# A two-layer attention and gated-delta backbone on one core: the block inversion in two parts, the second layer's modulation moved to the first layer's MLP, and small matmuls kept together by tile

## The chip, the cores and the metric

The kernel runs on one core of one Trainium2 chip. The metric is the device time of one execution in microseconds, median of several runs. Five engines work side by side, each through its own instruction list in order: TensorE (PE, matmuls and transposes; PEld are its weight loads), VectorE (DVE), ScalarE (ACT), GpSimd (POOL) and SyncE (SP), which here issues nearly all DMAs. They wait for one another through semaphores.

## The reference, cut to what matters

A batch of 512 latent tokens (a 64-wide grid) and 256 context tokens, both 1024 wide, passes through two layers:

```python
def hybrid_layer(x, cx, cond, cond_ctx, ...):
    sh_a, sc_a, gt_a, sh_m, sc_m, gt_m = ada_mod(cond, w_mod, b_mod)   # silu(cond) @ w_mod + b_mod, (1024) -> 6 x 1024
    csh_a, ..., cgt_m                  = ada_mod(cond_ctx, w_mod, b_mod)
    a_qkv, a_z, a_beta, a_alpha, b_qkv, c_qkv = split_cols(modulate(x, g_attn, sh_a, sc_a) @ w_in)
    ...                                                     # the same for the context
    o_a, oc_a = gdn_mixer(...)                              # gated delta rule, 8 heads, both directions, chunks of 64
    o_b, oc_b = global_gqa(...)                             # 4 heads, all keys
    o_c, oc_c = window_gqa(...)                             # 4 heads, banded, with sinks
    x = x + gt_a * (jnp.concatenate([o_a, o_b, o_c], axis=-1) @ w_out)
    x = x + gt_m * sq_relu_mlp(modulate(x, g_mlp, sh_m, sc_m), w_mlp_in, w_mlp_out)   # relu(h @ w1)^2 @ w2, 4096 wide
    ...                                                     # the context too, in the first layer only

def gated_delta_chunked(q, k, v, g, beta, s0):              # per direction and head, chunk by chunk
    low = jnp.where(idx[:, None] > idx[None, :], einsum(kb, kc) * decay, 0.0)          # 64 x 64
    sol = triangular_solve(eye + low, rhs, lower=True, unit_diagonal=True)             # u, w
    v_new = u_i - w_i @ s;  s_new = s * exp(gl_i) + ke_i.T @ v_new                     # serial over the chunks
    o_i = q_i @ s + a_i @ v_new
```

The modulation of a layer is a product of a vector (two of them: latent and context condition) with a 1024 x 6144 matrix, 24 MB of weights. The triangular solve is done through the inverse of `eye + low`.

## The kernel before

**Recording and planning.** The Python code doesn't issue instructions. Each call such as `nc.tensor.matmul` records an operation with the tiles that it reads and writes (`Program.add`, L353). `Program.layout` (L428) then plans: it gives each operation a cost and a rank (the longest priced path from it to the end of the program), and runs a list scheduler over the five engines. At each step the engine that is free first takes, among its operations whose inputs are ready, the one of highest rank, if a buffer is free for it. `Program.issue` (L639) emits the instructions in the order found. So the order on each engine, DMA issues included, follows from costs, ranks and buffer counts, and a small edit can move instructions anywhere. All instructions are emitted from one line, L683, so the trace is read by tile names, not by lines.

**Buffers.** `KINDS` (L36) lists the kinds of tiles, with columns, whether the type is fp32r, and five counts of slots: kept all the time, in region X in phases 0 and 1 of a layer, in region X in phase 2, and the same for region Y. Phase 0 of a layer is its input projection, phase 1 the scans and attention, phase 2 the output projection and the MLP. A region is opened for its next phase when all tiles of the one before are done. `sm` holds a 128x1024 piece (512 KB) of `w_mod`: two slots, in phases 0 and 1 alone. `x` and `h` (the residual and the hidden activations) live in region X of phase 2. `ps` and `pu` are the eight PSUM banks, five and three. `st` and `w` are raw weights and their split into two fp32r halves (ACT makes the high part, DVE the low part).

**Dense work.** Each projection multiplies with three fp32r products (`mm3`, L796): 24 matmuls of 512 columns for the latent tokens and 24 of 256 columns for the context per 128x1024 weight piece. The trace has them as `ps<-b,w` (projections, first MLP matrix), `ps<-w,b` (head projections) and `ps<-h,w` (second MLP matrix).

**Modulation** (`mod_steps`, L822). The six vectors of a layer are computed in three steps r = 0, 1, 2 of two vectors each. A step loads 16 pieces of `w_mod` into `sm` and runs four matmuls per piece, 128 rows by 32 columns (`ps<-sm,cs`, eight records per piece), into one `ps` bank; then ACT copies the bank, PE transposes it and DVE adds the bias. Step 0 is needed by a layer's first norm, steps 1 and 2 by its output projection and its MLP. Before the change, `run` records steps 1 and 2 of layer l, and step 0 of layer l + 1, after the attention of layer l, that is in phase 1.

**The scan.** For each of two head groups g there are six units u, each one 128-row system per direction. `system` (L1466) builds A and stores it to memory; `invert` (L1500) loads the 16x16 diagonal blocks of all six units as rows of one tile (96 partitions: 16 rows per unit), and inverts them together on DVE by 22 pairs of a product (`u<-iv,iv`) and a reduction (`iv<-u`); the result goes to memory as `Z`. `pre` (L1530) loads a unit's part of `Z` (`q<-Z`), which POOL spreads into a tile `s`, and completes the inverse by small matmuls of 32x32 and 64x32 blocks (`pu<-s,u`, `pu<-s,s`). Two `scan_step`s per unit follow, a serial chain of matmuls of 64x64 blocks (`pu<-v,u`, `pu<-u,kv`, `pu<-u,kaq`) and DVE, ACT and POOL work. `key_products` (L1443) makes the 64x64 products of keys and queries (`ps<-g`, `ps<-g,g`).

**What sets the order around the change.** `units` (L1730) records system 0 to 5, one inversion, then pre and scan unit by unit. PE takes matmuls by rank, one at a time: two products that go to different tiles, and are ready together, alternate.

Of the kernel before, what the change touches and what calls it, by code (L numbers as in the profile page):

```python
# [33 lines left out]


KINDS = {  # L36
# [267 lines left out]
PE, ACT, DVE, POOL, SP = range(5)  # L304
# [3 lines left out]
WINDOW = 4096 / 1.2  # L308
COLD = 0.36
WARM = 0.66  # L310
TABLES = {AF.Exp: 0, AF.Tanh: 0, AF.Ln: 1}


class Program:
# [113 lines left out]
    def layout(self):  # L428
        ops = self.ops
# [10 lines left out]
        for k, l in chains.items():  # L440
            n = KINDS[k][2] + KINDS[k][3] + max(KINDS[k][5:])
# [43 lines left out]
        clock, avail, future = [0.0] * 5, [[] for _ in range(5)], [[] for _ in range(5)]  # L485
        parked = {k: [] for k in KINDS}
        queues, front, order, table = 0.0, 0, [], 0
        warm, work, spill, window = False, 0.0, 0.0, 0
        done = bytearray(len(ops) + 1)
        for o in ops:  # L490
            if not o.wait:
                heapq.heappush(future[o.eng], (0.0, o.n))
# [40 lines left out]
        while len(order) < len(ops):  # L533
# [5 lines left out]
            if best is None and early:  # L539
                n = heapq.heappop(early)[1]  # L540
# [5 lines left out]
            t, e = best  # L546
            now = max(now, t)
            while future[e] and future[e][0][0] <= t:
                n = heapq.heappop(future[e])[1]
                heapq.heappush(avail[e], (-ops[n].rank, n))  # L550
            n = heapq.heappop(avail[e])[1]
            o = ops[n]
            if longest - o.rank > AHEAD[e] and n != front and n not in forced and any(
                    x.slot is None and x.kind in HOARD for x in o.tiles):
# [23 lines left out]
            o.start = t  # L578
            end = t + o.dur
            if e == PE:  # L580

                w = int(t / WINDOW)
                while window < w:
                    warm = work > (COLD if warm else WARM) * WINDOW
                    work, window = spill, window + 1
                    spill = 0.0
                if not warm:
                    end += o.dur
                d = (end - t) * o.dense
                over = min(1.0, max(0.0, end - (w + 1) * WINDOW) / (end - t))  # L590
                work, spill = work + d * (1 - over), spill + d * over
# [10 lines left out]
            for s in o.succs:  # L602
                q = ops[s]
# [24 lines left out]
            while early and (longest + early[0][0] <= AHEAD[ops[early[0][1]].eng] or early[0][1] == front):  # L628
                n = heapq.heappop(early)[1]
# [79 lines left out]
class Model:  # L709
# [236 lines left out]
        return xs, y  # L946

    @job("mlp")
    def mlp(self, L, who, xs, y, W, after=None):

        acc = dict.fromkeys(who)
        for q in range(4):
            hid = {i: [] for i in who}
            for s in range(KT):
                ps = self.fm_steps(self.weight(W.pop(0)), y, who)
                for i in who:
                    n = TOKENS[i]
                    r = self.g()
                    self.act(r[:, :n], ps[i][:, :n], AF.Relu)
                    hi, lo = self.pair("hid", i, s, "h")  # L960
                    self.act(hi, r[:, :n], AF.Square)
                    self.mul(r[:, :n], r[:, :n], r[:, :n])
                    self.tt(lo, r[:, :n], hi.bitcast(F32), ALU.subtract)
                    hid[i].append((hi, lo))
            for j in range(KT):
                ps = self.fm_steps(self.weight(W.pop(0)), hid, who)
                for i in who:
                    self.residual(L, xs[i], j, ps[i], i, 40)
                    if q == 3:
                        if after and i == LAT:  # L970
                            after(j, xs[i][j])
                        if not L.last:
                            acc[i] = self.norm_add(acc[i], xs[i][j], TOKENS[i])
        return acc
# [754 lines left out]

    def units(self, L, g, us):  # L1730
        if us and us[0] == 0:
            for u in range(6):
                self.system(L, u, g)
            self.invert(L, g, range(6))
        for u in us:
            self.pre(L, u, g)
            for st in (2 * u, 2 * u + 1):
                self.p.lead = LEAD[g]
                self.scan_step(L, g, st)
            ts = {1: () if L.last else (4, 5), 4: (1, 2), 5: (0, 3)}.get(u, ())  # L1740
            if ts:
                self.finish(L, ts, g)

    def run(self):
# [25 lines left out]
        for L in layers:  # L1770
# [14 lines left out]
            for i in reversed(who):  # L1785
                for nm, row in (("B", 4), ("C", 6)):
                    self.attention(L, nm, nm == "C", row, i)
            self.mod_steps(L, (1, 2))
            if not L.last:
                self.mod_begin(layers[L.l + 1])  # L1790
                self.mod_steps(layers[L.l + 1], (0,))
            self.enter(3 * L.l + 2)
            W = self.out_mlp_weights(L.l)
            xs, y = self.out_proj(L, who, W, x2 if L.last else self.a["xT"])
            if L.last:
                self.mlp(L, who, xs, y, W, lambda j, x: nc.sync.dma_start(self.out[:, j, :], x))
            else:
                acc = self.mlp(L, who, xs, y, W)
                x2 = self.p.tile("dram x2", (P, KT, NL), F32, None)
                for k in range(KT):  # L1800
                    nc.sync.dma_start(x2[:, k, :], xs[LAT][k])
                y = {i: self.norm_end(acc[i], layers[L.l + 1], 0, i, xs[i]) for i in (CTX, LAT)}
# [19 lines left out]
```

## Time and profile before

| | us |
|---|---|
| median of 3 runs (2345.0 to 2347.67) | 2345.96 |
| the profiled execution | 2335.23 |
| its span, first to last instruction | 2333.4 |
| PE busy | 2119.1 (91% of the span) |
| DVE busy | 1214.4 (52%) |
| ACT busy | 878.4 (38%) |
| POOL busy | 358.0 (15%) |
| mean granted TensorE clock | 0.929 of full speed |

The program passes, in order, through phases 0 and 1 of the first layer (to about 710 us of the span), its output projection and MLP (to about 1320), phases 0 and 1 of the second layer (to about 1910), and its output projection and MLP. In the rows further down a window is "start:end, length, busy time of each engine (instructions), granted TensorE clock, busy share of the DMA engines, GB/s". A line of a timeline is "start, length, engine, line, operation, output<-inputs, shapes, type, count", and in brackets the idle time of the engine before it and who ended it. Equal instructions that follow each other are merged in one line. Lengths of matmuls overlap, so what a piece of work costs PE is read as the distance from its start to the next line's start.

### The profile page before, as it was taken

What the parts mean: (1) busy time and instruction counts of PE and PEld (TensorE: products, weight loads), DVE (VectorE), ACT (ScalarE), POOL (GpSimd) and SP (SyncE); (2) the same over time, 40 slices, a digit from 0 to 9 for tenths busy, and PEclk for the clock granted to TensorE, in tenths of its full rate; (3) what the DMA queues carried; (4) which work ended last, traced back from release to release, by engine and by line L of the source; (5) the groups of instructions that cost most, each with busy time, mean ns of one, the idle gap of its engine ahead of it and who ended that gap; (6) DMA issues with size and microseconds to landing.
All of it is one profiled execution on the core that took longest, in us unless ns stands there. A gap on an engine that the chain in (4) does not pass through costs nothing.

```text
span 2333.4 us, 45381 instructions
## 1 busy us (share of the span) xinstructions
PE 2119.1 (91%) x18584; PEld 1690.0 (72%) x18584; DVE 1214.4 (52%) x2481; ACT 878.4 (38%) x1717; POOL 358.0 (15%) x392
## 2 busy tenths in 40 slices
PE   5899999679989899999999888989869988999999
PEld 2687788446657788888888767678636766878777
DVE  4668547765653632332333485757754655334333
ACT  4736325336432521312222363543425444222321
POOL 0133323432320000000000012244411310000000
PEclk9888899779998999999999997979769989999999
DMA  7267425894763121221221327466675532322322
GB/s 276 83 183 201 118 77 160 250 296 123 213 214 115 46 73 57 77 72 46 73 66 66 95 78 195 130 186 200 204 207 160 165 97 69 102 91 99 100 91 82
DMA packets 250224, 305.49 MB, mean 131 GB/s; under 512 B 97952, under 2 KB 172704, under 8 KB 250016
## 3 DMA queue, kind: packets, MB, share of 16 engines
q1 hardware_dynamic: 250016, 302.59, 43.0%
q8 instruction: 146, 2.39, 0.4%
q14 instruction: 62, 0.51, 0.1%
HBM read 246.32 MB, written 56.20 MB: 130 GB/s over the span
## 4 chain that ended last, share of the span: by engine, by line
PE 72%; DVE 9%; DMA 8%; ACT 4%; issue 3%; SPq 2%; POOL 2%; DVEq 0%; ACTq 0%; POOLq 0%
PE ps L683 65%; PE pu L683 7%; DVE g L683 3%; DMA sm<-w_mod 2%; SPq L683 2%; ACT g L683 2%; DVE t L683 2%; DVE u L683 2%; ACT L683 1%; DVE w L683 1%; POOL u L683 1%; DMA u<-kk 1%; DMA u<-xT 1%; DMA st<-w_qkv 1%; ACT u L683 1%
## 5 line engine op out<-in xcount | busy, mean ns | idle before, releaser
L683 PE MATMUL ps<-b,w 128*128 128x512 f32 (+1 forms) x3936 | 832.2, 363 | 22.4 <-ACT b L683 10.6
L683 PEld LDWEIGHTS ps<-b,w 128*128 128x128 f32 x3936 | 661.7, 193 | 151.9 <-ACT b L683 13.4
L683 PE MATMUL ps<-h,w 128*128 128x512 f32 (+1 forms) x2304 | 476.0, 356 | 1.9 <-DVE w L683 0.9
L683 PEld LDWEIGHTS ps<-h,w 128*128 128x128 f32 x2304 | 381.3, 188 | 70.7 <-DVE w L683 4.9
L683 ACT ACTIVATE w<-st 128x1024 fp32r<-128x1024 f32 x192 | 198.1, 1055 | 600.9 <-PE ps L683 598.9
L683 DVE TENSOR_TENSOR w<-st,w 128x1024 fp32r<-128x1024 f32 x192 | 234.7, 1250 | 245.0 <-PE ps L683 177.1
L683 ACT ACTIVATE g<-ps 128x512 f32<-128x512 f32 (+4 forms) x334 | 164.7, 514 | 267.9 <-PE ps L683 265.7
L683 DVE SCALAR_TENSOR_TENSOR x<-ps,mod,x 128x512 f32<-128x512 f32 (+1 forms) x120 | 77.3, 659 | 276.7 <-PE ps L683 276.6
L683 PE MATMUL ps<-w,b 128*128 128x256 f32 x1536 | 214.0, 292 | 1.1 <-ACT g L683 0.7
L683 PEld LDWEIGHTS ps<-w,b 128*128 128x128 f32 x1536 | 196.3, 195 | 5.8 <-ACT g L683 1.1
L683 PE MATMUL ps<-sm,cs 128*32 128x256 f32 x688 | 88.6, 465 | 42.0 <-DMA sm<-w_mod 36.3
L683 DVE TENSOR_TENSOR g<-g 128x512 f32<-128x512 f32 (+3 forms) x112 | 57.9, 542 | 125.5 <-ACT h L683 118.9
L683 DVE SCALAR_TENSOR_TENSOR g<-ps,par,g 128x510 f32<-128x510 f32 (+3 forms) x176 | 104.0, 620 | 31.9 <-ACT g L683 31.3
L683 PE MATMUL ps<-cst,g 128*128 128x128 f32 (+1 forms) x502 | 95.7, 307 | 21.2 <-ACT g L683 16.4
L683 POOL MEMSET iv<- 96x64 f32 (+1 forms) x12 | 5.5, 454 | 675.1 <-DVE g L683 657.9
L683 ACT ACTIVATE g<-ps,t 128x256 f32<-128x256 f32 (+2 forms) x144 | 75.2, 529 | 75.8 <-DVE t L683 70.5
L683 PEld LDWEIGHTS ps<-cst,g 128*128 128x128 f32 (+1 forms) x502 | 60.9, 152 | 50.4 <-ACT g L683 28.5
L683 PE MATMUL ps<-g,g 128*64 128x128 f32 (+1 forms) x1056 | 92.1, 294 | 5.7 <-DVE g L683 3.7
L683 DVE TENSOR_REDUCE t<-ps 128x2 f32<-128x512 f32 (+3 forms) x104 | 62.8, 623 | 60.9 <-PE ps L683 58.3
L683 PE MATMUL pu<-u,kaq 64*64 64x64 f32 (+1 forms) x1344 | 90.5, 248 | 2.6 <-DVE u L683 1.7
L683 DVE TENSOR_TENSOR g<-g,g 128x512 f32<-128x512 f32 (+3 forms) x129 | 76.6, 627 | 28.6 <-ACT g L683 24.2
L683 PEld LDWEIGHTS pu<-u,kaq 64*64 64x64 f32 (+1 forms) x1344 | 66.9, 152 | 25.8 <-issue 9.5
(131 smaller groups left out, 2326.8 us busy)
## 6 DMA issues: line engine op xcount, KB each, us to landing
st<-w SPq DMA_DIRECT2D x128, 512.0 KB
sm<-w_mod SPq DMA_DIRECT2D x86, 512.0 KB
st<-w_qkv SPq DMA_DIRECT2D x24, 512.0 KB
st<-w_tm SPq DMA_DIRECT2D x24, 512.0 KB
kv<-kv SPq DMA_DIRECT2D x96, 128.0 KB
u<-gd SPq DMA_DIRECT2D x88, 128.0 KB
u<-kk SPq DMA_DIRECT2D x88, 128.0 KB
kaq<-kq SPq DMA_DIRECT2D x80, 128.0 KB
```

The source lines that it names most:

```text
L683: getattr(engines[o.eng], o.name)(*[real(x) for x in o.args], **{k: real(x) for k, x in o.kw.items()})
```

## The change

Three edits, all in what is recorded and how it is ordered; the computation is the same, and so is the number of matmuls.

1. **Inversion in two parts.** `units` builds the systems of units 0 and 1, inverts them, then builds those of units 2 to 5 and inverts those. Each inversion runs the same 22 pairs on DVE, on 32 and on 64 partitions where it was one on 96.
2. **Second layer's modulation in the first layer's MLP.** `sm` gets one slot in region X of phase 2. The first layer's phase 1 records only its own steps 1 and 2; the second layer's steps 0, 1 and 2 are recorded at the start of the first three quarters of the first layer's MLP. The second layer's phase 1 has none.
3. **Small matmuls of a tile together.** The planner remembers the PSUM tile of the last matmul on PE if that matmul fills less than `FULL` = 0.9 of the array (`dense`: rows of the contraction over 128, times 0.6 for 64 columns or fewer), and takes a ready matmul into the same tile before one of higher rank. The modulation's matmuls have 128 rows and 256 columns, so for them `dense` is 1.0 and the rule doesn't apply.

```diff
-    "sm": (1024, False, 0, 2, 0, 0, 0),
+    "sm": (1024, False, 0, 2, 1, 0, 0),
...
+FULL = 0.9
...
+        group = None
...
             n = heapq.heappop(avail[e])[1]
+            if e == PE and ops[n].args[0].tile is not group:
+
+                d = [x for x in avail[e] if ops[x[1]].args[0].tile is group]
+                if d:
+                    d = min(d)
+                    avail[e].remove(d)
+                    heapq.heapify(avail[e])
+                    heapq.heappush(avail[e], (-ops[n].rank, n))
+                    n = d[1]
             o = ops[n]
...
             if e == PE:
+                group = o.args[0].tile if o.dense < FULL else None
...
-    def mlp(self, L, who, xs, y, W, after=None):
+    def mlp(self, L, who, xs, y, W, after=None, beside=None):
...
             hid = {i: [] for i in who}
+            if beside and q < 3:
+                self.mod_steps(beside, (q,))
...
         if us and us[0] == 0:
-            for u in range(6):
-                self.system(L, u, g)
-            self.invert(L, g, range(6))
+            for part in (range(2), range(2, 6)):
+                for u in part:
+                    self.system(L, u, g)
+                self.invert(L, g, part)
...
-            self.mod_steps(L, (1, 2))
-            if not L.last:
-                self.mod_begin(layers[L.l + 1])
-                self.mod_steps(layers[L.l + 1], (0,))
+            if L.l == 0:
+                self.mod_steps(L, (1, 2))
...
-                acc = self.mlp(L, who, xs, y, W)
+                self.mod_begin(layers[L.l + 1])
+                acc = self.mlp(L, who, xs, y, W, beside=layers[L.l + 1])
```

PE, second layer, where the attention starts (`ps<-a,a` scores, `ps<-cst,g` transposes, `ps<-g,g` outputs) and unit 0 of head group 1 is completed (`pu<-s,u`, 32 matmuls, then `pu<-s,s`). Before:

```order
L683 MATMUL pu_140<-s_14918,u_11614 32x32 x17
L683 MATMUL ps_137<-a_14928,a_11633 128x512 x2
L683 MATMUL ps_139<-cst,g_14917 128x128
L683 MATMUL pu_140<-s_14918,u_11614 32x32 x2
L683 MATMUL ps_136<-g_14916,g_115 64x128 x4
L683 MATMUL pu_140<-s_14918,u_11614 32x32
L683 MATMUL ps_138<-sm_11600,cs 32x256 x4
L683 MATMUL pu_140<-s_11604,s_11603 32x32 x29
```

After, the same unit; its neighbours are now the transposes of the head projections (`ps<-cst,r`):

```order
L696 MATMUL ps_137<-cst,r_11911 128x128 x2
L696 MATMUL pu_142<-s_15825,u_11891 32x32 x32
L696 MATMUL pu_140<-u_15827,kaq_15833 64x64 x7
L696 MATMUL pu_142<-s_11880,s_11879 32x32 x32
L696 MATMUL ps_137<-cst,r_11911 128x128 x4
L696 MATMUL pu_142<-s_15825,u_11891 64x32 x16
```

The 32 matmuls stand in five pieces before and in one after, no modulation is among them, and the unit is completed ahead of the attention, not within it. Counted over the two orders, matmuls into `pu` of 64 rows or fewer stand in 541 pieces before and 313 after (first layer 267 and 152, second 274 and 161), those into `ps` in 309 and 185 (162 and 103, 147 and 82).

PE, first layer's MLP, `h` the hidden activations. Before, dense matmuls alone:

```order
L683 MATMUL ps_138<-h_7273,w_109 128x512
L683 MATMUL ps_137<-h_7269,w_112 128x512
L683 MATMUL ps_135<-h_7267,w_112 128x256
L683 MATMUL ps_139<-h_7266,w_109 128x256
L683 MATMUL ps_135<-h_7267,w_112 128x256
```

After, at the start of modulation step 1 of the second layer, and in step 0:

```order
L696 MATMUL ps_136<-b_7296,w_112 128x512 x2
L696 MATMUL ps_136<-b_7296,w_110 128x512
L696 MATMUL ps_137<-sm_7228,cs 32x256 x4
L696 MATMUL ps_139<-h_7229,w_108 128x512 x2
L696 MATMUL ps_139<-h_7229,w_113 128x512
```

```order
L696 MATMUL ps_138<-sm_7228,cs 32x256
L696 MATMUL ps_139<-b_7290,w_110 128x256
L696 MATMUL ps_135<-b_7293,w_113 128x512
L696 MATMUL ps_138<-sm_7228,cs 32x256
L696 MATMUL ps_139<-b_7300,w_112 128x256
L696 MATMUL ps_138<-sm_7228,cs 32x256
L696 MATMUL ps_139<-b_7300,w_112 128x256
L696 MATMUL ps_135<-b_7293,w_113 128x512
L696 MATMUL ps_138<-sm_7228,cs 32x256
```

48 pieces of `w_mod` pass through the one `sm` slot here. Between one piece's matmuls and the next stand as a rule some 21 dense matmuls of 512 columns, or as much in other widths; in steps 1 and 2 the four of a piece stand together, in step 0 (which begins in the output projection) five pieces are broken up, nine cuts in all.

SP, second layer, head group 1: the store of the inverted blocks (`Z<-iv`) and the loads of the first attention (`a<-kB`). Before:

```order
L683 DMA Z_97<-iv_11632 96x1024
L683 DMA sm_11601<-w_mod 128x1024
L683 DMA kC_103<-r_11635 512x1x128
L683 DMA a_14928<-kB_100 128x2x512
L683 DMA a_14929<-qB_99 128x2x512
L683 DMA a_14930<-kB_100 128x2x512
L683 DMA q_14924<-Z_97 64x8x16 x2
```

After, the first part's store and reload, and (62 rows further on) the attention's loads:

```order
L696 DMA Z_97<-iv_11907 32x1024
L696 DMA iv_11908<-A_95 8x63x16 x3
L696 DMA q_11900<-Z_97 64x8x16 x2
L696 DMA iv_11908<-A_95 8x63x16 x3
L696 DMA q_11901<-Z_97 64x8x16 x2
```

```order
L696 DMA a_15835<-kB_100 128x2x512
L696 DMA kaq_11904<-B_96 64x512
L696 DMA a_15836<-qB_99 128x2x512
```

The first units' blocks are stored 65 rows ahead of the attention's loads, where the one store stood three rows ahead of them.

## Rows read from the trace of the kernel before

**Rows 1.** Windows by stage: length, busy of PE, PEld, DVE, ACT, POOL, clock, DMA, GB/s.

```profile
120.00:400.00 280.00, 262.88 (x2829) 228.86 (x2826) 180.12 (x334) 120.30 (x217) 90.89 (x80) 0.91 0.53 149
400.00:540.00 140.00, 101.67 (x1204) 66.92 (x1204) 91.98 (x251) 54.74 (x147) 51.72 (x50) 0.78 0.89 260
540.00:690.00 150.00, 139.96 (x2610) 99.63 (x2604) 89.81 (x294) 73.62 (x219) 42.77 (x50) 1.00 0.60 179
690.00:710.00 20.00, 9.04 (x57) 3.04 (x58) 5.19 (x23) 3.47 (x7) 1.01 (x2) 0.59 0.80 258
710.00:1320.00 610.00, 603.61 (x3415) 524.64 (x3415) 227.95 (x346) 165.49 (x266) 0.00 (x0) 0.99 0.20 66
1320.00:1690.00 370.00, 321.22 (x3472) 264.38 (x3470) 259.23 (x504) 170.07 (x316) 113.71 (x124) 0.87 0.58 161
1690.00:1740.00 50.00, 29.07 (x210) 14.90 (x209) 27.98 (x74) 10.09 (x23) 10.75 (x10) 0.57 0.73 216
1740.00:1910.00 170.00, 159.01 (x2621) 112.27 (x2613) 95.80 (x317) 84.61 (x246) 38.91 (x45) 0.95 0.47 139
```

**Rows 2.** PE's waits from 690 to 710 us: us in total, times, longest.

```profile
PE ps L683 <- DMA sm<-w_mod: 8.8, 5, 3.7
```

**Rows 3.** The chain that ended last, 685 to 712 us: start, us, what.

```profile
689.69 4.84 DMA sm<-w_mod
...
694.58 1.13 PE ps L683 x8
...
701.76 4.07 DMA sm<-w_mod
```

**Rows 4.** Timeline of PE, first layer, scans and attention.

```profile
665.57 0.63 PE L683 MATMUL ps<-sm,cs 128*32 128x256 f32 x4
666.13 0.68 PE L683 MATMUL pu<-u,kaq 64*64 64x64 f32 x14
...
667.29 0.75 PE L683 MATMUL pu<-s,u 32*32 32x32 f32 x64
667.97 0.33 PE L683 MATMUL ps<-cst,g 128*128 128x128 f32 x1
668.23 0.62 PE L683 MATMUL ps<-sm,cs 128*32 128x256 f32 x2
668.78 0.68 PE L683 MATMUL pu<-v,u 64*64 64x64 f32 x16
```

**Rows 5.** Timeline of PE, second layer, unit 0 of head group 1.

```profile
1739.76 0.42 PE L683 MATMUL pu<-s,u 32*32 32x32 f32 x10 [2.23 <-POOL s L683]
1740.11 1.11 PE L683 MATMUL ps<-cst,g 128*128 128x128 f32 x4
...
1745.66 0.50 PE L683 MATMUL pu<-s,u 32*32 32x32 f32 x34
1746.09 0.73 PE L683 MATMUL ps<-a,a 128*128 128x512 f32 x2
...
1746.86 0.25 PE L683 MATMUL pu<-s,u 32*32 32x32 f32 x4
1747.04 0.66 PE L683 MATMUL ps<-g,g 128*64 128x128 f32 x8
```

**Rows 6.** Windows of the instructions on sm alone: PE, PEld, clock, DMA, GB/s.

```profile
1690.00:1740.00 50.00, 10.76 (x76) 2.27 (x76) 0.57 0.73 216
1740.00:1910.00 170.00, 21.07 (x152) 5.20 (x152) 0.95 0.47 139
```

**Rows 7.** Windows of the instructions on iv alone, the four inversions' sum: DVE, POOL.

```profile
sum 570.00, DVE 77.86 POOL 3.14; mean DVE 19.46 POOL 0.79
```

**Rows 8.** Timelines of SP and POOL, second layer, before unit 0 of head group 1.

```profile
1725.59 0.34 SPq L683 DMA_DIRECT2D Z<-iv  x1
1732.11 3.37 SPq L683 DMA_DIRECT2D q<-Z  x4
```

```profile
1739.10 0.61 POOL L683 TENSOR_TENSOR s<-q,cst 128x256 f32<-128x256 f32 x1 [27.88 <-DMA q<-Z]
```

**Rows 9.** Timeline of PE, where the first layer's output projection starts.

```profile
709.58 35.81 PE L683 MATMUL ps<-b,w 128*128 128x512 f32 x202 [0.79 <-ACT b L683]
```

2 rows, old and new, of the table KINDS are left out of this document.

## The prediction

> **What bounds the kernel now.** I read the windows by stage first [rows 1], then who ends PE's waits, then single lines of the timeline. The kernel has two sorts of stages. In the first layer's output projection and MLP (710 to 1320 us) PE is busy 603.61 of 610 us at a clock of 0.99, so whatever is added to PE there lengthens the run by its own length. In phases 0 and 1 PE is busy 262.88 of 280, 101.67 of 140, 139.96 of 150, 9.04 of 20 us in the first layer, and 321.22 of 370, 29.07 of 50, 159.01 of 170 in the second. So most of these stages is PE's too, but in two holes, at 400 to 540 and 1690 to 1740 us, PE idles for 38 and 21 us and the granted clock falls to 0.78 and 0.57 [rows 1]. The second hole can be followed: DVE's inversion of head group 1 ends, `Z` is stored at 1725.59, reloaded from 1732.11, POOL spreads it at 1739.10 after an idle of 27.88 us [rows 8], and PE takes it at 1739.76 [rows 5]. At 690 to 710 us PE has nothing but the last pieces of `w_mod`; 8.8 us of waiting go to them [rows 2], and the chain that ended last runs through their loads [rows 3].
>
> **Small matmuls together.** What a cut costs is read from the distance to the next start. Unit 0's 64 records of 32x32 products in one piece take 667.97 - 667.29 = 0.68 us; pieces of 10, 34 and 4 take 0.35, 0.43 and 0.18 [rows 4, 5]. A line through these is about 0.17 us per piece and 0.008 us per record. I take 0.2 us per cut, since the 64x64 products are longer at the start (14 records in 0.6 us or less). The orders have 115 cuts fewer into `pu` in the first layer and 113 in the second, 23 us each. Of the 59 and 65 fewer cuts into `ps` most are key products, of which no line here shows the price apart; I take 0.1 us, 6 us each, between 0 and the 0.2 above. Where PE idles a cut costs nothing: PE is busy 0.87 of these stages, less in the holes, so I count three quarters: **-22 us in each layer**. Bounds: 0, if other engines set the pace, and -45, where the clock is at its low level and a cut costs double.
>
> **The modulation taken out.** Step 0 of the second layer leaves the first layer's phase 1, 16 pieces. A piece between other work costs about 0.56 us whether it has 2, 4 or 8 records (666.13 - 665.57, 668.78 - 668.23) [rows 4]. Ten pieces lie in filled stretches: -5.7 us. Six stand at 690 to 710 us, where PE only waits for their loads [rows 2, 3]; but the scan's end, its store and the reload of the mix run at the same time, and the other 32 pieces stay in the phase. Of the 20 us I take half, -10, bounds 0 and -19. In the second layer all 32 leave. Those in the hole (10.76 us busy at 0.57 of the clock) were fillers and are worth nothing; those after 1740 us are 152 records, 19 pieces, 21.07 us busy as an upper bound and 19 x 0.56 = 10.6 as a lower [rows 6]: **-14 us**. What hides behind them: nothing, PE takes the next attention or scan product.
>
> **The modulation put into the MLP.** 48 pieces on a full engine. At the warm clock 0.56 us per piece between other small work [rows 4], 1.13 at the low clock [rows 3]. In the MLP each one stands between dense matmuls, a pair that this trace does not show, so I take 0.75: 36 us. Nine cuts of step 0 at 0.56 add 5 us, three closings (four transposes behind each step) 2 us. Then the loads: with one slot, a piece is loaded only after the matmuls of the one before. A load takes 4.07 to 4.84 us [rows 3]. Meanwhile PE has some 21 dense matmuls; 202 of mixed width took 35.81 us [rows 9], 0.177 each, hence about 0.236 for one of 512 columns and 5.0 us for 21. The two nearly balance, and where an `st` load runs at the same time the load is late; I take 0.1 us per piece, 5 us. **+48 us**, bounds 27 (0.56 each and nothing else) and 130 (2.7 us per piece, the distance of such pieces at 690 to 710 us).
>
> The Trainium skill, "TensorEngine Tiling (Array Packing)", section Key Properties, says that a change of tiling mode drains TensorE. It speaks for the grouping and against these 48 pieces, each of which changes the mode twice. That a piece of 2 records costs as much as one of 8 agrees with it; the page has no price, and the sum would be the same by it, since 0.75 lies above the row's 0.56.
>
> **The inversion in two parts.** It adds 88 pairs of DVE instructions, since an instruction's length follows its columns, and these are the same on 32, 64 or 96 partitions. The four inversions took 77.86 us of DVE [rows 7], so +39 us in each layer, and four more stores, 12 more POOL memsets and their waits, all in engines that are busy under 0.75 of these stages (DVE 259.23 of 370, POOL 113.71 of 370) [rows 1]. DVE also splits the weights for PE in these stages, in order, so a part comes through: I take 6 us of 39 per layer, bounds 0 and 39. In return the first two units need no longer wait for the systems of the other four. In the order of SP the first `Z` of the second layer's head group 1 stands 65 rows ahead of the attention's loads, before it was three, and PE completes unit 0 among the transposes of the head projections. So the scan fills the hole, and what comes next there is the attention, which then runs without it at the end of the phase. Second layer: idle 21 us and 29 us of busy time at 0.57 of the clock, of which I take **-14**, bounds 0 and -35; first layer, where the hole is also a DMA queue at 0.89 [rows 1] and the attention's own chains, **-10** of 38, bounds 0 and -38.
>
> **The sum.** First layer, phases 0 and 1: -22 - 5.7 - 10 - 10 + 6 = -42. MLP: +48. Second layer: -22 - 14 - 14 + 6 = -44. The second MLP is untouched. Together -38 against the profiled execution of 2335, that is 2297; the median of the runs lies 11 us above the profiled one, so 2346 - 38 = **2308 us** for the median after.
>
> **The rivals.** *The loads of the MLP set PE's pace.* If each piece lands 1.5 us behind the matmul that needs it, because the `st` loads share the queue, 48 x 1.5 = 72 us less the 5 counted come on top: -38 + 67 = +29, 2375 us, slower. It decides from 0.9 us per piece on (43 us). For it: a full engine that runs in order, one slot, loads of 4.07 to 4.84 us beside 5.0 us of cover. Against it: a DMA share of 0.20 there [rows 1], and a load that is late only if others run with it. *DVE becomes the bound in phases 0 and 1.* With all 78 us on the path in place of 12, +28, 2374 us. For it, DVE's 74 instructions and 27.98 us in the hole at 1690, just before PE is fed [rows 1]; against it, DVE idles a third of these stages. Half of it on the path gives -11, 2335. *The cuts cost nothing*, because PE's stretches with scans are paced by the chain through DVE and ACT, and the grouping only lets lower ranks pass: the 44 us go, +6, 2352, at the edge of what can be told from no change. For it, the serial scan; against it, 159.01 of 170 us busy. *More than forecast:* the scan fills both holes wholly and the clock stays up: 24 more from the holes, 12 without the DVE toll, 10 on the pieces at 0.56, so -84, 2262 us.
>
> **How the numbers follow.** The forecast, 2262 to 2341, has 0.66. More than that 0.10. No change, within 0.2% (4.7 us, about what a measurement of this kernel tells from none), 0.08: the costless cuts or half of DVE's toll. Slower 0.16: the late loads 0.07, DVE 0.05, the costless cuts with dearer pieces 0.04. So faster 0.76, same 0.08, slower 0.16. A range from 2258 to 2362 leaves out about 0.1 on either side.
>
> **What would show it.** The window of the first MLP longer by 40 to 55 us, with `sm` pieces of 0.56 to 0.8 us between dense matmuls, and PE waiting for `sm` there under 10 us; 50 or more would be the first rival. The hole before the second layer's attention at under 30 us, its scan of head group 1 starting before the first `ps<-a,a`. Small products of a unit in one line of the timeline of 0.6 to 0.7 us. PE's busy time lower by 20 us or more in all. At the end of the first layer's phase 1 no wait for `sm` of 8 us. DVE busy up by about 78 us. Wrong it would be if phases 0 and 1 got no shorter though PE's work in them did: then the waits of PE there name DVE tiles, or the attention stands alone at the end and PE idles.

## The result, and the profile after

The changed kernel takes 2310.94 us (median of 4 runs, 2301.45 to 2314.42), the kernel before 2345.48 beside it. The ratio is 0.985 with an interval of 0.982 to 0.989, so the change is worth 35 us; the forecast was 38. The profiled execution took 2314.42 us, its span 2312.3, at a mean clock of 0.921.

The stage table below carries the rest of this text. A stage ends where a row of PE's timeline says so: "layer 1" runs from the start to the first unbroken `ps<-b,w` of the first output projection, "MLP 1" to the last `ps<-h,w` of the first MLP, "layer 2" to the first `ps<-b,w` of the second output projection, "rest" to the last `ps<-h,w`. Each row is one profiled execution, so a difference carries the scatter of two. The profiled execution of the kernel before is 10 us faster than its median, those of the other kernels lie within 8 us of theirs; the stage "MLP 1" agrees within 1.4 us in all kernels without the move, so the scatter lies in the other stages. Against "before" the rows therefore come out up to 18 us too high in sum, mostly some 10 (-21 here, where the medians give -35).

| kernel | layer 1 | MLP 1 | layer 2 | rest |
|---|---|---|---|---|
| before | 709.6 | 619.2 | 580.6 | 419.4 |
| after | 687.1 | 667.4 | 528.1 | 425.1 |
| difference | -22.5 | +48.2 | -52.5 | +5.7 |
| forecast | -42 | +48 | -44 | 0 |

The windows by stage of the kernel after (columns as in [rows 1]):

```profile
120.00:400.00 280.00, 244.91 (x2953) 211.67 (x2957) 207.78 (x413) 122.38 (x223) 97.13 (x86) 0.88 0.56 158
400.00:540.00 140.00, 101.15 (x1553) 77.49 (x1549) 107.61 (x266) 50.98 (x133) 71.47 (x68) 0.77 0.76 218
540.00:687.00 147.00, 136.22 (x2036) 95.06 (x2036) 90.18 (x308) 80.72 (x237) 28.22 (x32) 0.94 0.61 179
687.00:1354.00 667.00, 657.21 (x3843) 542.26 (x3844) 235.28 (x371) 169.32 (x271) 0.00 (x0) 0.99 0.32 103
1354.00:1720.00 366.00, 314.19 (x3990) 263.45 (x3991) 297.43 (x630) 179.21 (x334) 135.06 (x140) 0.90 0.59 162
1720.00:1770.00 50.00, 34.77 (x684) 26.55 (x680) 30.01 (x83) 13.74 (x38) 15.25 (x19) 0.60 0.57 150
1770.00:1883.00 113.00, 103.53 (x1323) 78.56 (x1323) 71.02 (x252) 70.04 (x209) 23.00 (x25) 0.93 0.26 75
```

Beside [rows 1] three things are to be seen. The MLP is still full: PE is busy 657.21 of 667 us. The first layer's hole at 400 to 540 us is as it was: 101.15 busy of 140 at 0.77, before 101.67 at 0.78. The second layer's hole is narrower and no warmer: 34.77 of 50 at 0.60, before 29.07 at 0.57. Over the whole stages, layer 1 is shorter by 29.5 us of PE's busy time and longer by 7.0 us of its idle time (113.7 before, 120.7 after); layer 2 is shorter by 49.1 us of busy and 3.4 us of idle time (79.9 and 76.5). So nearly all that the change gains there is work of PE, not waiting.

What PE waits for in the first MLP, from the list of its waits (us in total, times, longest); no `sm` is among them:

```profile
PE ps L696 <- ACT b L696: 6.3, 2, 3.6
PE ps L696 <- DVE w L696: 2.0, 3, 0.9
PE ps L696 <- ACT g L696: 1.4, 3, 0.7
PE ps L696 <- DVE amul L696: 0.6, 1, 0.6
```

How a modulation piece lies there, from the timeline of PE:

```profile
706.72 0.64 PE L696 MATMUL ps<-sm,cs 128*32 128x256 f32 x8
707.29 7.50 PE L696 MATMUL ps<-b,w 128*128 128x512 f32 x32
714.72 0.63 PE L696 MATMUL ps<-sm,cs 128*32 128x256 f32 x4
715.27 0.49 PE L696 MATMUL ps<-b,w 128*128 128x512 f32 x1
715.70 0.63 PE L696 MATMUL ps<-sm,cs 128*32 128x256 f32 x4
716.25 0.73 PE L696 MATMUL ps<-b,w 128*128 128x512 f32 x2
```

From start to next start a whole piece (eight records) takes 0.57 us and half a piece (four records, one of the cuts of step 0) 0.55. A dense matmul beside a piece takes longer than one among its like: the lone one between the two halves 0.43 us, the 32 in a row 0.23 each. All instructions on `sm` in this stage, and those on `iv` in the whole run (one window each, PE and DVE busy):

```profile
687.06:1354.50 667.44, 36.18 (x376) 0.99 0.32 103
```

```profile
0.00:2312.00 2312.00, 158.03 (x352) 0.92 0.44 132
```

376 records are 47 pieces, 0.77 us of busy time each with their cuts; the trace has them in 56 rows. The inversions take 158.03 us of DVE where they took 77.86 [rows 7]. The second layer's head group 1: the first row below is unit 0, the first of the first part, to be held against [rows 5]; the other three are unit 2, the first of the second part:

```profile
1682.57 0.75 PE L696 MATMUL pu<-s,u 32*32 32x32 f32 x64
...
1742.42 1.08 PE L696 MATMUL pu<-s,u 32*32 32x32 f32 x64 [1.26 <-POOL s L696]
1743.43 1.11 PE L696 MATMUL pu<-u,kaq 64*64 64x64 f32 x14
1744.47 1.07 PE L696 MATMUL pu<-s,s 32*32 32x32 f32 x64
```

The products stand together, 64 records in 0.69 us (1683.26 - 1682.57) and, for unit 2 at the low clock, in 1.01. The listing ahead that is called "the same unit" after the change has the sequence of rows of unit 2, not of unit 0. Unit 0 comes 328.1 us after the end of the first MLP, before the change 411.0 (1739.76 - 1328.8), so 83 us earlier, and 82 us ahead of the attention (1764.5), before 4 us behind it. The scan now ends at 1846 and the attention alone at 1873; before, both ended at 1895.

This early start did not take the idle time away. Ahead of unit 0, from 1640 to 1682 us, PE is busy 26.43 of 42 us. Its longest wait there, 6.27 us up to 1660.91, is for weights (`w`) that DVE splits; DVE, busy 27.38 us of 1640 to 1670, runs the pairs of the first part's inversion meanwhile and makes that `w` from 1659.65 on. Then PE waits again, ahead of unit 2. Where there was one hole, each part of the inversion has one of its own.

### The profile page after: what moved, and what is told of

Its sections match the earlier page's. It is cut to its first block, busy times and chain, and to the rows that moved or that the text cites. A ratio compares the mean times of both kernels' runs of the same rounds, so it can differ in the third digit from the quotient of the medians.

```text
span 2312.3 us, 45635 instructions
## 1 busy us (share of the span) xinstructions
PE 2086.6 (90%) x18584; PEld 1670.7 (72%) x18584; DVE 1274.1 (55%) x2657; ACT 879.8 (38%) x1719; POOL 377.9 (16%) x404
## 4 chain that ended last, share of the span: by engine, by line
PE 68%; DVE 14%; DMA 7%; issue 4%; ACT 4%; SPq 2%; POOL 2%; DVEq 0%; ACTq 0%; POOLq 0%
PE ps L696 62%; PE pu L696 5%; DVE g L696 4%; DVE u L696 3%; DVE t L696 3%; ACT g L696 2%; SPq L696 2%; DMA sm<-w_mod 1%; DVE iv L696 1%; DVE w L696 1%; ACT L696 1%; DMA kB<-r 1%; DMA u<-xT 1%; DVE v L696 1%; DMA kv<-kv 1%
## 5 line engine op out<-in xcount | busy, mean ns | idle before, releaser
L696 PE MATMUL ps<-b,w 128*128 128x512 f32 (+1 forms) x3936 | 849.0, 366 | 33.1 <-ACT b L696 13.7
L696 ACT ACTIVATE g<-ps 128x512 f32<-128x512 f32 (+3 forms) x334 | 164.9, 516 | 250.0 <-PE ps L696 230.8
L696 PE MATMUL ps<-w,b 128*128 128x256 f32 x1536 | 217.5, 292 | 11.2 <-DVE w L696 8.5
L696 PEld LDWEIGHTS ps<-w,b 128*128 128x128 f32 x1536 | 196.4, 194 | 16.5 <-DVE w L696 8.9
L696 POOL MEMSET iv<- 32x64 f32 (+3 forms) x24 | 10.8, 451 | 797.3 <-DVE g L696 733.6
L696 DVE TENSOR_TENSOR u<-iv,iv 32x256 f32<-32x256 f32 (+27 forms) x176 | 90.6, 515 | 6.1 <-POOL iv L696 4.1
L696 PEld LDWEIGHTS ps<-cst,g 128*128 128x128 f32 (+1 forms) x502 | 61.3, 151 | 42.7 <-ACT g L696 23.5
L696 PE MATMUL ps<-sm,cs 128*32 128x256 f32 x688 | 73.9, 429 | 19.5 <-DMA sm<-w_mod 13.7
L696 DVE TENSOR_TENSOR g<-g,g 128x512 f32<-128x512 f32 (+3 forms) x129 | 71.3, 578 | 31.3 <-ACT g L696 27.4
L696 DVE TENSOR_REDUCE t<-ps 128x1 f32<-128x512 f32 (+3 forms) x104 | 63.2, 625 | 40.4 <-PE ps L696 39.4
L696 ACT ACTIVATE g<-g 128x512 f32<-128x512 f32 (+2 forms) x123 | 65.2, 552 | 45.9 <-DVE g L696 23.5
```

Of the source, the lines that this page charges most:

```text
L696: getattr(engines[o.eng], o.name)(*[real(x) for x in o.args], **{k: real(x) for k, x in o.kw.items()})
```

## The experiments

The theory under test is the prediction's sum: each part has its own price, and the prices add up. The rivals are its own: late loads, DVE as the bound, cuts that cost nothing. A run of one part, of two and of all three gives eight kernels; each part can then be priced alone and beside the others. All ratios are to the kernel before, timed on the same chip.

**One part alone, and all but the grouping.** The edits are pieces of the diff ahead:

```diff
# e1_inv
+            for part in (range(2), range(2, 6)):
# e2_mod
+            if beside and q < 3:
+                self.mod_steps(beside, (q,))
# e3_grp
+                group = o.args[0].tile if o.dense < FULL else None
# e4_inv_mod: the first two together
```

> Only the inversion in two parts, on the kernel before. My theory: two times +6 for DVE's added 39 us, less 10 and 14 for the holes that the scan fills, together -12: a ratio of about 0.995, the hole before the second layer's attention at under 30 us. Rival, DVE becomes the bound: most of the 78 us on the path, +20 to +54, ratio 1.01 to 1.02.

> Only the modulation's move, on the kernel before. My theory: +48 in the first MLP, -16 in the first layer and -14 in the second, together +18: ratio about 1.008. If the second layer's pieces were worth more than I counted (the profile of the changed kernel had that stage 52 us shorter in place of 44), the sum is nearer to +8. Rival, late loads in the MLP: +60 or more in that window.

> Only the small matmuls of a tile together, on the kernel before. My theory: -22 in each layer, together -44, ratio about 0.981, and PE busy about 30 us less. Rival, the cuts cost nothing because the scan's chain through DVE and ACT sets the pace: PE busy 30 us less, its waits as much more, time within 5 us of before.

> Inversion in two parts and the modulation's move, without the grouping. My theory: the whole change of -38 without the grouping's -44, so +6, ratio about 1.003. Rival, the grouping is worth nothing: -35 as the whole change, ratio 0.985. Stage by stage, the first MLP should be as long as with the whole change, and phases 0 and 1 about 22 us longer in each layer.

Measured against 2345.23 us: the split alone 2358.66, ratio 1.005 (1.003 to 1.008); the modulation's move alone 2324.04, 0.993 (0.990 to 0.995); the grouping alone 2301.65, 0.983 (0.980 to 0.986); split and move without grouping 2367.32, 1.010 (1.007 to 1.013). In us, by the medians, +13, -21, -44, +22 (the ratios differ from these by up to 4 us). The grouping's time came out as forecast; that PE's busy time would fall by about 30 us did not, it fell by 64. The other two came out with the wrong sign, by 25 us to the bad and 39 to the good. And they don't add up: -8 was to be expected of the two together, and +22 was measured.

| kernel | layer 1 | MLP 1 | layer 2 | rest |
|---|---|---|---|---|
| split | 742.0 | 619.1 | 572.1 | 424.8 |
| move | 676.5 | 662.3 | 551.6 | 422.1 |
| grouping | 700.7 | 618.9 | 550.7 | 422.3 |
| split, move | 730.2 | 663.1 | 545.8 | 421.2 |

The move alone costs 43 us in the MLP and gives back 33 in layer 1 and 29 in layer 2, not 16 and 14. The windows of phases 0 and 1 say how; the kernel before first, then the one with the move, then the one with the grouping (first and second layer each):

```profile
200.00:710.00 510.00, 438.62 (x6161) 332.71 (x6160) 305.56 (x799) 218.03 (x534) 153.81 (x156) 0.89 0.63 183
1329.00:1909.00 580.00, 500.46 (x6244) 384.04 (x6243) 376.20 (x884) 261.72 (x578) 163.38 (x178) 0.86 0.56 159
```

```profile
200.00:676.00 476.00, 422.15 (x6027) 326.55 (x6025) 306.60 (x790) 216.62 (x532) 154.65 (x156) 0.90 0.61 174
1339.00:1890.00 551.00, 488.07 (x5981) 396.55 (x5979) 367.93 (x874) 259.08 (x576) 163.51 (x178) 0.84 0.49 138
```

```profile
200.00:701.00 501.00, 414.50 (x6164) 318.79 (x6163) 305.95 (x800) 214.74 (x532) 155.78 (x156) 0.86 0.64 187
1320.00:1870.00 550.00, 461.08 (x6243) 363.42 (x6243) 372.46 (x884) 262.49 (x580) 165.53 (x178) 0.88 0.58 168
```

With the grouping alone PE's busy time falls by 24 and 39 us, and its idle time rises by 15 and 9. With the move alone PE's busy time falls by 16 and 12 us, about what I had counted in all; its idle time falls as well, by 17.5 (71.4 to 53.9) and 16.6 us (79.5 to 62.9). The waits for the modulation's loads in the kernel before, over the whole of those two stages, were as much as that:

```profile
PE ps L683 <- DMA sm<-w_mod: 14.7, 10, 3.7
...
PE ps L683 <- DMA sm<-w_mod: 11.0, 6, 2.8
```

With the move alone they are 0.6 and none.

**Two parts with the grouping, the split in one layer, and DVE's work by itself.**

```diff
# e5_mod_grp, e6_inv_grp: pieces of the diff ahead
# e7_split2, on e5
+            for part in ((range(2), range(2, 6)) if L.last else (range(6),)):
# e8_dve2, on the kernel before
         nc.sync.dma_start(L.Z[g, 16 * us[0]:16 * us[0] + n], X[:n])
+        for i in range(1, BASE):
+            for k, j in ([(0, i + 1)] if i < hb else [(0, i)] + [(hb, i + 1)] * (i > hb)):
...
+                self.mul(tmp, xt[:, :, k:k + hb, k:j],
...
+                nc.vector.tensor_reduce(lb[:, :, 0, 0:hb], tmp, axis=AX.X, op=ALU.add)
```

> The whole change without the split of the inversion. If the parts add up as they measured alone (the modulation's move -17, the grouping -40), -57: about 2288, better than the whole change by 20 us or more, and the first layer's phases 0 and 1 about 15 to 30 us shorter than with the whole change. Rival, my prediction's theory: the split is worth 12 us in the whole change, so 2320 here. Second rival: the split only costs where the cuts are not grouped, then the time of the whole change within 5 us.

> The whole change without the modulation's move. By the parts alone (+13 and -40): -27, about 2318, 7 us slower than the whole change. By my prediction's terms (+48 - 30 = +18 taken out of the whole change): 2290, 20 us faster than the whole change.

> Grouping and modulation's move, with the inversion split in the second layer only. The split alone cost 32 us in the first layer's phases 0 and 1 and gave 8 back in the second's. If that holds beside the other two parts, this is the fastest: about 8 us under the kernel without any split. Rival: the split's cost is DVE's work, in either layer, then it lies half way between the kernel without a split and the whole change, or slower.

> The kernel before with DVE's added work alone: after each inversion has stored its result, its multiplications and sums run once more into space that nothing reads, 39 us of DVE in each layer, as much as the split adds; the inversion is not split, nothing waits for the added work. If DVE's work is what made the split cost 32 us in the first layer, the first layer's phases 0 and 1 grow by 20 to 40 us and the run by 13 to 40. If the cost comes from the order that the split brings (the scan's small products earlier, among the projections, at a lower clock), it stays within 5 us of before, with DVE busy 78 us more.

Measured against 2345.95 us: move and grouping 2293.25, ratio 0.979 (0.975 to 0.983); **split and grouping 2272.14, 0.969 (0.966 to 0.973)**; the split in the second layer only 2300.14, 0.980 (0.976 to 0.985); DVE's work alone 2355.36, 1.005 (1.003 to 1.007). Move and grouping came 5 us from the 2288 that the parts add up to. Of split and grouping neither the parts (2318) nor my terms (2290) told the time. The split in the second layer only was to be the fastest, 8 us under move and grouping, and is 7 us above: its rival, half way to the whole change, came out. DVE's work alone cost the run less than the 13 to 40 us of its theory and more than the 5 of its rival.

| kernel | layer 1 | MLP 1 | layer 2 | rest |
|---|---|---|---|---|
| move, grouping | 670.6 | 667.5 | 530.5 | 425.3 |
| split, grouping | 691.1 | 619.8 | 536.7 | 416.3 |
| move, grouping, split in layer 2 | 664.3 | 666.1 | 544.0 | 424.2 |
| before, with DVE's added work | 733.1 | 619.6 | 576.7 | 418.4 |

So the whole change is beaten by two of its parts by 39 us. What each part is worth depends on its company: the split +13 alone, -30 beside the grouping, +18 beside grouping and move (2311 against 2293). The move -21 alone, +39 beside grouping and split. The grouping is worth 31 to 87 us, whatever stands beside it. (2311 against 2293 is at the limit of what these runs tell apart, the ends of their intervals overlap; the 39 us are well beyond it.)

Why the move no longer pays stands in the stages: it costs 47.6 in the MLP as before, but gives back 4.0 us in layer 1 and 8.6 in layer 2. Another 8.8 us lie in the last stage, where both kernels record the same. Windows of split and grouping, and of the whole change in the first layer:

```profile
200.00:691.00 491.00, 421.58 (x6190) 323.85 (x6188) 328.49 (x889) 221.38 (x541) 162.35 (x162) 0.88 0.67 192
1311.00:1848.00 537.00, 463.51 (x6247) 362.00 (x6245) 406.56 (x973) 264.37 (x582) 171.99 (x184) 0.90 0.61 173
```

```profile
200.00:687.00 487.00, 410.40 (x6058) 322.02 (x6056) 343.75 (x884) 222.26 (x539) 166.09 (x162) 0.87 0.61 173
```

In the first layer PE's busy time falls by 11.2 us when step 0 leaves, and its idle time rises by 7.2. The longest waits of PE in these stages of the first layer, with split and grouping:

```profile
PE pu L696 <- DVE u L696: 14.6, 9, 4.2
PE ps L696 <- DMA sm<-w_mod: 14.1, 8, 4.5
PE ps L696 <- DVE r L696: 10.6, 6, 3.6
PE ps L696 <- ACT g L696: 10.2, 14, 2.1
PE pu L696 <- DVE v L696: 5.2, 3, 3.8
PE ps L696 <- DVE g L696: 2.7, 3, 2.0
```

and with the whole change:

```profile
PE ps L696 <- ACT g L696: 18.3, 18, 3.8
PE pu L696 <- DVE u L696: 11.0, 9, 5.6
PE pu L696 <- DVE v L696: 10.0, 6, 3.6
PE ps L696 <- DVE g L696: 8.4, 3, 7.7
PE pu L696 <- issue: 4.5, 3, 3.5
PE ps L696 <- DMA sm<-w_mod: 3.4, 2, 2.5
PE ps L696 <- DVE r L696: 3.3, 4, 1.3
```

Summed over all rows of the two lists, the waits for the modulation's loads fall by 10.7 us; those for ACT rise by 10.5, for POOL by 3.0, "issue" by 4.3, and those for DVE stay (less for `r` and `u`, more for `g` and `v`). PE waits 74.9 us in place of 67.8.

Where the new waits lie tells more. From 200 to 300 us no modulation matmul runs in either kernel, and yet PE is idle there for 22.3 us with the whole change and for 13.4 with split and grouping:

```profile
200.00:250.00 50.00, 37.31 (x740) 29.65 (x738) 40.34 (x93) 24.19 (x45) 24.98 (x24) 0.84 0.57 152
250.00:300.00 50.00, 40.41 (x531) 28.73 (x532) 24.65 (x51) 24.01 (x42) 14.39 (x13) 0.72 0.56 149
...
200.00:250.00 50.00, 41.88 (x744) 31.47 (x742) 38.10 (x82) 30.75 (x54) 18.03 (x18) 0.86 0.67 156
250.00:300.00 50.00, 44.76 (x580) 36.92 (x581) 33.88 (x69) 21.19 (x42) 12.25 (x12) 0.91 0.45 123
```

(the whole change first). Split and move without grouping have 19.5 us there, the split alone 12.5, and no kernel without the split over 11. With the whole change the longest wait in it is one of 7.7 us for a `g` of DVE. So in layer 1 a split inversion and the move together bring a wait of their own, in a stretch from which no modulation was taken; it must come with the new order, and which step of the plan makes it was not tested. From 300 us on the waits for the loads that go (10.7 us) are nearly all replaced by others: the idle time falls by only 1.8 us. By kernels, the move's return in layer 1 is 33 us alone and 30 beside the grouping, but 12 beside the split and 4 beside both.

DVE's work alone, whose results nothing reads, costs 23.5 us in layer 1 (733.1 against 709.6) and nothing in layer 2 (-4), +19 over the four stages. The runs give +9, so about half of it is the fast profiled execution of before. The split alone has +32 in layer 1, +29 over the stages and +13 in the runs. The window shows DVE's work as busy time of PE, not as waiting:

```profile
200.00:733.00 533.00, 460.74 (x6165) 345.09 (x6163) 339.20 (x889) 217.37 (x535) 156.56 (x158) 0.86 0.60 175
```

The same matmuls (6165, before 6161) take 22 us more at a clock of 0.86 for 0.89, the idle time is 1 us more. But they do not stand in the same order: the planner placed the added work too, and in the trace the matmuls into `pu` of layer 1 lie in 303 stretches of one kind where they lay in 277, those of layer 2 in 246 for 295 (with the split alone 310 and 249). At 0.2 us per cut this is +5 and -10 us, the signs of the two stages. Nor is the clock of the one execution typical: over its runs the kernel before had mean clocks of 0.911 to 0.932, the profiled one 0.929; the kernel with DVE's work had 0.908 to 0.922. So this run does not tell DVE's load from the order that came with it.

**DVE's work beside the grouping, what an order is worth, and a third slot.**

```diff
# e9_dve2_grp: e8 and the grouping
# e10_inv_grp_order on e6, e11_after_order on the kernel after
-WARM = 0.66
+WARM = 0.68
# e12_inv_grp_sm3, on e6
-    "sm": (1024, False, 0, 2, 0, 0, 0),
+    "sm": (1024, False, 0, 3, 0, 0, 0),
```

> DVE's added work without the split, as in the run before, now beside the grouping. If DVE's 39 us per layer lengthen the first layer's phases 0 and 1 only where PE's small matmuls are not grouped, this comes within 5 us of the kernel with the grouping alone (2302), the first layer at 491 to 506 us of phases 0 and 1. If DVE's work costs the same beside the grouping, that stage is about 23 us longer than with the grouping alone and the run about 10 to 25.

> Split and grouping, without the modulation's move, and one constant of the planner's cost model 3% larger: the same instructions, in another order. It measures what an order alone is worth. If the 39 us between this kernel and the whole change belong to the modulation's place, this stays within 10 us of 2272. If they are luck of an order, it lands anywhere between 2272 and 2311.

> The whole change with the same constant 3% larger, to the same end. If the modulation's place is the cause, it stays within 10 us of the whole change (2311) and at least 20 us behind the run above. If it is an order's luck, the two come near each other.

> Split and grouping, modulation left in phases 0 and 1 with a third slot for its loads there. PE waited 14 and 9 us for these loads in the two layers' stages. If they were late because a slot came free late, those waits go and the run gains 10 to 20 us on 2272. If the waits are only what is left when nothing else is ready, other waits take their place and the time stays within 10 us.

Measured against 2339.56 us: DVE's work with the grouping 2294.58, ratio 0.979 (0.975 to 0.984); split and grouping in another order 2280.76, 0.974 (0.969 to 0.978); the whole change in another order 2309.27, 0.986 (0.981 to 0.991); the third slot 2295.26, 0.979 (0.975 to 0.984).

| kernel | layer 1 | MLP 1 | layer 2 | rest |
|---|---|---|---|---|
| DVE's work, grouping | 709.7 | 619.3 | 543.6 | 418.6 |
| split, grouping, other order | 689.6 | 618.4 | 551.0 | 419.9 |
| all, other order | 689.7 | 666.3 | 519.7 | 423.2 |
| split, grouping, third slot | 688.4 | 619.3 | 557.2 | 422.9 |

Beside the grouping DVE's added work costs the run nothing (2294.58, the grouping alone 2301.65): 9 us in layer 1, less than nothing in layer 2. There the number of such stretches hardly changes (160 and 163, 156 and 160). The orders move the run by 8.6 and by 1.7 us; 28.5 of the 39 us between the two kernels stay, so most of it stays with the modulation's place, the waits of 200 to 300 us among it (in the other order PE idles there for 22.4 us with the whole change and for 13.1 with split and grouping), and some is an order's luck. By stage the two orders differ by 2 and 3 us in layer 1, by 14 and 8 in layer 2. The kernel with the split in layer 2 alone records there the same work as the whole change, and takes 544.0 where that takes 528.1 and, in the other order, 519.7; in layer 1 it records the same as move and grouping, and takes 664.3 for 670.6. So in layer 1 differences of one stage mean something from 10 us on, in layer 2 only from some 25.

The third slot did not take the waits for the loads away:

```profile
PE ps L696 <- DMA sm<-w_mod: 17.5, 9, 4.7
```

in layer 1 (before 14.1), 8.6 in layer 2 (9.4). Layer 1 is 2.7 us shorter, layer 2 20 us longer, the run 23 us. A third slot does not bring the loads in time. Whether the 20 us in layer 2 are more than an order's luck stays open.

## Why the prediction was right, and where it was right by luck

The time was right (2308 forecast, 2311 measured). Of its steps:

- **Small matmuls together, -22 in each layer: right.** Alone it gave 44 us, the whole of the forecast, in the stages -9 and -30, so the two layers together were right and each by itself was not. PE's busy time in them fell by 24 and 39 us (438.2 to 414.2, 500.7 to 461.4); the counted cuts at their prices were 29 in each. Counting the cuts in the order and pricing one by the distance to the next start held as a sum. Of the 64 us of work that went, 24 came back as waits, where a quarter had been allowed for. The rival that cuts cost nothing falls, since the time fell.
- **The modulation into the MLP, +48: right in the sum and in the price of a piece.** The stage is 48.2 us longer. A whole piece takes 0.57 us from start to start, the 0.56 of [rows 4], and not 0.75; but the dense matmuls right before and behind one take 0.33 and 0.34 us where the others take 0.23 (medians, 512 columns), so that a piece costs PE 0.57 + 0.2 = 0.77. Over 56 rows that makes up for the 9.4 us by which PE's busy time outside the pieces rose (657.7 - 612.1 - 36.2); the nine cuts are part of the 36.2. Waits rose by 2.6, none of them for `sm`, for 5 of late loads. The rival of the late loads falls.
- **The modulation out, -15.7 and -14: the step that failed, on both sides.** I priced the pieces by PE's busy time alone, gave the waits in the first layer half of the last 20 us and left them out in the second, since pieces in a hole "were fillers and are worth nothing". Alone the move gave back 33 and 29 us: the rows of the waits over the whole stage, 14.7 and 11.0 us, belonged into the sum, and I had read them for 20 us of it only [rows 2]. Beside the other two parts it gave 4 and 9: in layer 1 other waits replaced those for the loads, and with the split inversion there came 9 us of new waits from 200 to 300 us, where no piece had been. The forecast of 30 lies between 62 and 13, neither of which it was worked out for.
- **The hole filled, -10 and -14: the second step that failed.** The scan does start earlier, 83 us in the second layer, but the first layer's hole holds 38.9 us of idle time for 38.3, the second's 15.2 for 20.9 at nearly the same low clock, and a new one lies ahead of unit 0 (15.6 us of idle time from 1640 to 1682). Against move and grouping alone, the whole change has 16 us more idle time in layer 1 and 5 less in layer 2. Beside the grouping without the move the step held: PE's idle time fell by 13 us in layer 1 (129.4 to 116.2) and 16 in layer 2 (89.3 to 73.4; in the other order 15 and 8). Only there the forecast's mechanism is seen; alone and in the whole change it is not.
- **DVE's toll, +6 in each layer: right in its sum, as far as can be told.** The work alone, with the order that came with it, cost the run 9 us for 12, and nothing beside the grouping. In the whole change PE is seen to wait for weights while DVE inverts, 8.5 us in two waits ahead of unit 0; in its other order the waits for `w` in layer 2 are 4.5 us in place of 11.9. The rival that DVE becomes the bound, with all 78 us on the path, falls.
- **The second MLP, 0:** +5.7 us, of which 4.9 are waits of PE. Over all kernels this stage lies between 416.3 and 425.3; what decides it stays open.

The total was better than its parts. The stages sum to -21, as the two profiled executions do (2335.23 and 2314.42); they were off by +20 in layer 1, -8 in layer 2 and +6 at the end. The medians differ by 35, since the profiled execution of before lies 10 us below its median and that of after 3 us above. That the forecast met 2311 so closely is luck: part by part, it had a split worth 12 us and a move that costs 18. In the company in which they stand, the split costs 18 and the move 39: the whole change is faster because of the grouping alone, worth 56 us there, 12 more than forecast. The best kernel found takes two of the three parts, split and grouping, and leaves the modulation where it was: 2272 us, 3.1% under the kernel before.

Two things are not settled. Why the split helps beside the grouping (-30: -9.6 in layer 1, -14.0 in layer 2, which is less than an order moves there, -6.0 in the last stage) and hurts beside grouping and move (+18, of which +16.5 in layer 1): the waits of 200 to 300 us are most of that layer's loss, 14 of 16 us of idle time, but what in the plan puts them there was not tested. And whether more work on DVE by itself lowers the granted clock of PE, or only the order that is planned with it, no run tells apart.

## What to carry to other kernels

Work that fills waits and work that makes them look alike in a busy time; before moving it off one stage, list what the consumer waits for there over the whole stage, and ask which other wait would take the place. When a wait appears after such a move, look whether the moved work lay there at all: here much of the new waiting stood where none had been. In a program whose order is planned anew after each edit, prices of parts don't add up: time the parts alone and in company before shipping them together, since a gain of the sum can hide a part that costs more than it brings. Time one neutral change of the order too, to know how many us of a stage are luck.

## What the runs showed that was not expected

Pushing a small matmul in between dense ones costs more beside it than its own row shows: 0.1 us on the dense matmul ahead and as much on the one behind. More work on DVE that nothing reads made the run 0.5% slower (0.3 to 0.7), in the profiles by PE's busy time, at a granted clock of 0.86 in place of 0.89; but the planned order changed with it, and beside the grouping the same work cost nothing. And a third buffer for a load that PE waits for made the kernel 23 us slower (2295 against 2272) without shortening those waits.
